# Small steps of a norm and of a softmax rewritten, and elementwise work moved from GpSimd to VectorE, in a two-layer encoder kernel

## The chip, the cores and the metric

The kernel runs on one core of one Trainium2 chip. A core has a matrix engine (TensorE, PE in the profile, with its weight loads shown as PEld), VectorE (DVE), ScalarE (ACT), GpSimd (POOL) and a queue that issues most DMAs (SyncE, SP). The engines share an on-chip memory, SBUF, of 128 partitions; PE writes its results to PSUM, eight banks that DVE and ACT can read and write. The metric is the device time of one execution in microseconds (us); lower is better.

## The reference

Two requests, a prompt of 512 tokens and a sample of 1024, go through two layers with the same weights. All numbers are float32.

```python
def trunk(x, p, ln1, w_in, sink, w_fmix, w_ao, w_fo, w_out, w_pe, ln_pg, w_pg, ln_f):
    h = x
    for i in range(DEPTH):                       # DEPTH = 2, D_MODEL = 1024
        z = rmsnorm(h, ln1[i]) @ w_in[i]         # 1024 -> 4352 columns
        q, k, v, ga, uf, gf, mga, mgf = jnp.split(z, SPLIT_IDX, axis=-1)
        ...                                      # partial rotary on q and k
        a = band_attention(q, k, v, sink[i]) * jax.nn.silu(ga)
        f = fourier_mix(uf, w_fmix[i]) * jax.nn.silu(gf)
        merged = jax.nn.sigmoid(mga) * (a @ w_ao[i]) + jax.nn.sigmoid(mgf) * (f @ w_fo[i])
        h = h + merged @ w_out[i]
        gate = jax.nn.sigmoid(rmsnorm(h, ln_pg[i]) @ w_pg[i])
        h = h + (p[i].astype(h.dtype) @ w_pe[i]) * gate
    return rmsnorm(h, ln_f)

# in band_attention, s holds one head's scores times 1/8, masked to |i-j| <= 128:
    m = jnp.maximum(jnp.max(s, axis=-1, keepdims=True), sk)
    e = jnp.exp(s - m)
    pr = e / (jnp.sum(e, axis=-1, keepdims=True) + jnp.exp(sk - m))
```

## The kernel before

The tokens lie in three chunks of 512: chunk 0 is the prompt, chunks 1 and 2, the pair, are the sample. Activations stand transposed, 128 channels by 512 tokens to a tile. Every product is made of three matmuls of rounded operands: each operand is split into a high part, a cast on ACT (`S.copy`, L86), and a low part, the difference (L87), on the engine that the caller names (`hi_lo`). Those two lines are most of what ACT, DVE and POOL do.

A layer runs these stages, one after the other on PE, with side work stepped in between by `run`:

- `project_prompt`: 34 weight tiles times chunk 0 (L98 to L100). `Weights` loads a tile two steps ahead and splits it one step ahead, in two halves, on the two engines in `engs`. In layer 0 these are POOL and DVE; the streams of all later stages name POOL twice. Beside it run the norm and the operands of the pair (`pair_made`), the prompt's attention and its Fourier mixing.
- `project_pair`: 17 pairs of weight tiles times both sample chunks by a scheme with seven products in place of eight (`Pair`, L231). For each pair four sums of weight blocks S1 to S4 are made (L208 to L215, on POOL) and seven blocks are split, their low parts by turns on POOL (four) and on DVE (three). Each product goes to one of three PSUM banks, which DVE and ACT empty (L238 to L260). The sample's attention runs beside it.
- `merge` for the prompt, then for the pair: the branches' projections with gates (L514 to L522, whose sum is on POOL), the output projection with the residual (L540) and the sum of squares for the next norm (L299, L300), and the gate with its embedding (L556 to L560). The sample's Fourier mixing runs beside the first of them.

`Norm` adds up squares tile by tile (L300, on POOL where the caller names no engine). `stats` has PE turn the sums to a 128x4 tile in a PSUM bank (L305) and finds 1/sqrt by an integer guess and three rounds of three small operations (L307 to L314), all in SBUF tiles. `scale` has PE spread the result over a bank (L320), and DVE copies it out (L322).

In `attention`, one unit is a block of 128 queries and one key-value head, with four query heads. For each head DVE adds the mask to the scores and takes the row maximum (L675), makes the bias of it, at most minus the sink (L678), and ACT takes the exponential with its row sum (L680). After four heads the sink's share is made and added (L683 to L685), the reciprocal taken (L686) and the rows scaled (L688).

What sets the order: the program is written as generators, and the framework's scheduler then orders each engine's instructions by times that it expects. Each engine runs its own list strictly in that order, so an instruction that waits holds up all behind it.

Of the kernel before, what the change touches and what calls it, by code (L numbers as in the profile page):

```python
# [10 lines left out]
F32 = mybir.dt.float32  # L11
# [7 lines left out]
P = 128  # L19
# [20 lines left out]
def trunk(ctx: ExitStack, tc: tile.TileContext, x, p, w_in, w_af, w_out, w_pe, w_pg, w_fm,  # L40
# [14 lines left out]
    def sbt(shape, dt, tag, bufs=None):  # L55
        return sb.tile(shape, dt, tag=tag, name=nm(tag), bufs=bufs or BUFS[tag])
# [27 lines left out]
    def hi_lo(hi, lo, src, lo_eng):  # L84

        S.copy(hi, src)  # L86
        lo_eng.tensor_tensor(lo, src, f(hi), op=ALU.subtract)  # L87
# [93 lines left out]
    class Pair:  # L181
# [19 lines left out]
        def prepare(self, n):  # L201

            for b in range(len(self.w), min(n + 1, 7 * (len(self.sources) // 2))):
                p, i = divmod(b, 7)
                a, name = self.a[p], self.ORDER[i]
                if name == "S2":
                    a["S1"], a["S2"] = sbt([P, 4, P], F32, "scr"), sbt([P, 4, P], F32, "scr")
                    G.tensor_tensor(a["S1"], a["A21"], a["A22"], op=ALU.add)  # L208
                    G.tensor_tensor(a["S2"], a["S1"], a["A11"], op=ALU.subtract)
                elif name == "S3":  # L210
                    a["S3"] = sbt([P, 4, P], F32, "scr")
                    G.tensor_tensor(a["S3"], a["A11"], a["A21"], op=ALU.subtract)
                elif name == "S4":
                    a["S4"] = a["S2"]
                    G.tensor_tensor(a["S4"], a["A12"], a["S2"], op=ALU.subtract)  # L215
                t = wt([P, 2, 4, P], F32R)
                hi_lo(t[:, 0], t[:, 1], a[name], V if i % 2 else G)
                self.w[b] = [(t[:, 0, k, :], t[:, 1, k, :]) for k in range(4)]

        def steps(self, p, x, finish, lead):  # L220
# [68 lines left out]
    class Norm:  # L289
        def __init__(self):  # L290
            self.acc = None

        def add(self, h, eng=G):
            if self.acc is None:
                self.acc = scr()
                S.activation(self.acc, h, AF.Square)
            else:
                sq = scr()
                S.activation(sq, h, AF.Square)  # L299
                eng.tensor_tensor(self.acc, self.acc, sq, op=ALU.add)  # L300

        def stats(self):
            st = pst("misc")
            for j in range(4):
                PE.matmul(st[:, j : j + 1], self.acc[:, j * P : (j + 1) * P], mean_sb, start=True, stop=True)  # L305
            v, r, z = (sbt([P, 4], F32, "tiny") for _ in range(3))
            V.tensor_scalar(v, st[:, 0:4], EPS, None, op0=ALU.add)  # L307

            V.tensor_scalar(r.bitcast(I32), v.bitcast(I32), 1, None, op0=ALU.arith_shift_right)
            V.tensor_scalar(r.bitcast(I32), r.bitcast(I32), -1.0, float(0x5F3759DF), op0=ALU.mult, op1=ALU.add)  # L310
            for _ in range(3):
                V.scalar_tensor_tensor(z, r, -0.5, r, op0=ALU.mult, op1=ALU.mult)
                V.tensor_tensor(z, z, v, op=ALU.mult)
                V.scalar_tensor_tensor(r, z, 1.5, r, op0=ALU.add, op1=ALU.mult)  # L314
            self.r = r

# [182 lines left out]
    def merge(l, chunks, parts, ws, bank, groups):  # L499
# [3 lines left out]
        for m in range(KD):  # L503
            w = ws.get()
            for c in chunks:
                ga, gf = scr(), scr()
                SY.dma_start(ga, GT[c][2 * m])
                SY.dma_start(gf, GT[c][2 * m + 1])
                ao, fo = bank(), bank()
                mm3(ao, w[:4], parts[c][:4])  # L510
                tick()
                yield
                mm3(fo, w[4:], parts[c][4:])
                V.scalar_tensor_tensor(ga, ga, 1.0, ao, op0=ALU.add, op1=ALU.mult)  # L514
                V.scalar_tensor_tensor(gf, gf, 1.0, fo, op0=ALU.add, op1=ALU.mult)
                if len(chunks) == 1:
                    G.tensor_tensor(gf, ga, gf, op=ALU.add)
                    outs[c].append(two(halves(gf, V)))
                else:
                    if m % 2 == 0:  # L520
                        merged[c].append(big([P, 2, T]))
                    G.tensor_tensor(merged[c][-1][:, m % 2, :], ga, gf, op=ALU.add)  # L522
                yield
        if len(chunks) > 1:
            for c in chunks:
# [106 lines left out]
    def attention(l, chunks, slim):  # L632
# [25 lines left out]
        def scores(u):  # L658
            c, b, kv = units[u]
            qb, k0, k1 = window(c, b)  # L660
            W = (k1 - k0) * P
            msk = mask_sb[:, (k0 - qb + 1) * P : (k1 - qb + 1) * P]
            q, kw = blocks[c, b][kv]["q"], blocks[c, b][kv]["kw"]
            mx, nmx, rs, es, rd = (sbt([P, 4], F32, "stat") for _ in range(5))
            probs = []
            for i in range(4):
                head = 4 * kv + i
                sc = pst("sc")
                for j in range(2):
                    PE.matmul(sc[:, :W], q[:, i, :], kw[:, j, :], start=j == 0, stop=j == 1)  # L670
# [4 lines left out]
                V.tensor_tensor_reduce(out=pr, in0=sc[:, :W], in1=msk, scale=1.0, scalar=-3.0e38,  # L675
                                       op0=ALU.add, op1=ALU.max, accum_out=mx[:, e])

                V.scalar_tensor_tensor(nmx[:, e], mx[:, e], -0.125, nsink_sb[:, l, head : head + 1],  # L678
                                       op0=ALU.mult, op1=ALU.min)
                S.activation(pr, pr, AF.Exp, bias=nmx[:, e], scale=0.125, accum_out=rs[:, e])  # L680
                if i % 2:
                    yield
            V.tensor_tensor(es, sink_sb[:, l, 4 * kv : 4 * kv + 4], nmx, op=ALU.add)  # L683
            S.activation(es, es, AF.Exp)
            V.tensor_tensor(rd, rs, es, op=ALU.add)  # L685
            V.reciprocal(rd, rd)  # L686
            for i, pr in enumerate(probs):
                S.activation(pr, pr, AF.Copy, scale=rd[:, i : i + 1])  # L688
            blocks[c, b][kv]["probs"] = probs

        def values(u):
# [53 lines left out]
    def fourier(l, s):  # L745
# [68 lines left out]
        for g in range(4):  # L814
# [61 lines left out]
            o = tile([P, n_tok])  # L876
            V.tensor_copy(o[:, 0:1], s1[:, 0:1])
            V.tensor_tensor(o[:, 1 : quart + 1], s1[:, 1:], t1, op=ALU.subtract)
            G.tensor_tensor(o[:, 3 * quart :], s1[:, quart:0:-1], t1[:, ::-1], op=ALU.add)
            V.tensor_tensor(o[:, quart + 1 : half], s2[:, quart - 1 : 0 : -1], t2[:, quart - 2 :: -1], op=ALU.add)  # L880
            V.tensor_copy(o[:, half : half + 1], s2[:, 0:1])
            G.tensor_tensor(o[:, half + 1 : 3 * quart], s2[:, 1:quart], t2[:, : quart - 1], op=ALU.subtract)
            yield
            for i, c in enumerate(chunks):
                gu = gus[i]
# [222 lines left out]
```

## Time and profile before

| what | value |
|---|---|
| time, median of 3 runs | 2336.91 us (2334.51 to 2337.52) |
| profiled execution | 2336.8 us, its span 2334.6 us |
| PE busy | 2211.7 us, 10176 matmuls |
| DVE, ACT, POOL busy | 1424.6, 1088.9, 1113.4 us |

The span runs from the first to the last instruction; about 2.2 us lie outside it. Matmuls overlap in the profile, so PE's busy time is the time in which at least one is under way, and its idle time is the rest of the span, 122.9 us. The row PEclk of the page tells which share of full speed the chip granted to PE's clock. A row of a timeline reads: start, time from the first start to the last end, engine, line, operation, written tile, read tiles, sizes, number of instructions, and in brackets the idle time before and what ended it.

### The profile page before, as it was taken

Reading aid. Unit: us, or ns where it says so; the run is one execution under the profiler, and the core shown is the slowest. Engines: PE = TensorE matmul, PEld = TensorE weight load, DVE = VectorE, ACT = ScalarE, POOL = GpSimd, SP = SyncE. Lnnn points to the kernel's source line nnn. Section 1 sums busy time; section 2 is a strip of 40 time slices with the busy share of each in tenths; the row PEclk is TensorE's granted clock in tenths of the full one; section 3 lists DMA queues with packets and bytes.
Section 4 is the critical chain, followed back from the end, with each engine's and each line's share of the span. In section 5 each row is a group of like instructions: output and inputs, shape, how many; then the busy total and the mean of one; then the engine's idle time right before and its main releaser. Section 6 shows DMA issues by size and latency. Waiting matters only on the chain. (4 is left out here: it accounts for less than half of the span.)

```text
span 2334.6 us, 30544 instructions
## 1 busy us (share of the span) xinstructions
PE 2211.7 (95%) x10176; PEld 1812.2 (78%) x10176; DVE 1424.6 (61%) x2563; ACT 1088.9 (47%) x2292; POOL 1113.4 (48%) x827
## 2 busy tenths in 40 slices
PE   8899999999998989999999999899999999999986
PEld 6677777888877877888887787788787788788875
DVE  5866645677566775252767653657766666744376
ACT  5467433466664444223424853336666544422331
POOL 1313446444446863344514355644444568554471
PEclk9899999999999999999999999999999999999998
DMA  7565435445437464731445554453444655553232
GB/s 280 187 198 177 164 119 178 147 140 165 131 130 269 153 237 163 249 117 47 140 166 185 153 177 168 149 171 125 148 154 132 218 198 186 198 194 117 87 113 95
DMA packets 240542, 380.73 MB, mean 163 GB/s; under 512 B 21121, under 2 KB 95489, under 8 KB 240385
## 3 DMA queue, kind: packets, MB, share of 16 engines
q1 hardware_dynamic: 233472, 366.19, 46.6%
q10 hardware_dynamic: 6912, 12.59, 1.5%
q8 instruction: 81, 1.33, 0.2%
q14 instruction: 77, 0.62, 0.1%
HBM read 270.17 MB, written 108.53 MB: 162 GB/s over the span
## 5 line engine op out<-in xcount | busy, mean ns | idle before, releaser
L87 POOL TENSOR_TENSOR act<-act,act 128x512 fp32r<-128x512 f32 x386 | 547.2, 1437 | 463.4 <-ACT act L86 403.8
L231 PE MATMUL mm<-act,act 128*128 128x512 f32 x2856 | 700.4, 395 | 27.6 <-DVE act L87 11.7
L231 PEld LDWEIGHTS mm<-act,act 128*128 128x128 f32 x2856 | 531.1, 189 | 147.2 <-ACT act L86 18.0
L98 PE MATMUL mm<-act,act 128*128 128x512 f32 x1408 | 563.1, 400 | 29.6 <-ACT act L86 28.5
L100 PE MATMUL mm<-act,act 128*128 128x512 f32 x1408 | 559.3, 399 | 13.2 <-POOL act L87 13.2
L99 PE MATMUL mm<-act,act 128*128 128x512 f32 x1408 | 557.8, 396 | 0.0
L86 ACT CAST act<-act 128x512 fp32r<-128x512 f32 x574 | 330.1, 619 | 223.0 <-DMA act<-in_w_af 53.2
L98 PEld LDWEIGHTS mm<-act,act 128*128 128x128 f32 x1408 | 269.8, 192 | 88.6 <-ACT act L86 35.0
L100 PEld LDWEIGHTS mm<-act,act 128*128 128x128 f32 x1408 | 269.3, 191 | 78.2 <-POOL act L87 23.4
L99 PEld LDWEIGHTS mm<-act,act 128*128 128x128 f32 x1408 | 269.7, 192 | 54.0
L87 DVE TENSOR_TENSOR act<-scr,act 128x512 fp32r<-128x512 f32 x188 | 180.7, 979 | 102.8 <-ACT act L86 101.6
L86 ACT CAST act<-scr 128x512 fp32r<-128x512 f32 (+1 forms) x260 | 152.6, 614 | 170.8 <-DVE scr L382 79.0
L87 POOL TENSOR_TENSOR act<-scr,act 128x512 fp32r<-128x512 f32 (+1 forms) x72 | 100.1, 1392 | 207.6 <-ACT act L86 141.1
L87 DVE TENSOR_TENSOR act<-act,act 128x512 fp32r<-128x512 f32 x188 | 172.2, 944 | 35.7 <-ACT act L86 34.7
L300 POOL TENSOR_TENSOR scr<-scr,scr 128x512 f32<-128x512 f32 x67 | 94.5, 1411 | 173.5 <-ACT scr L299 164.1
L299 ACT ACTIVATE scr<-act 128x512 f32<-128x512 f32 x105 | 65.3, 632 | 236.8 <-DVE act L540 148.1
L680 ACT ACTIVATE act<-act,stat 128x384 f32<-128x384 f32 (+1 forms) x192 | 111.0, 580 | 68.9 <-DVE stat L678 68.5
L87 DVE TENSOR_TENSOR act<-misc,act 128x512 fp32r<-128x512 f32 x132 | 88.5, 687 | 76.8 <-ACT act L86 76.3
L86 ACT CAST act<-misc 128x512 fp32r<-128x512 f32 x132 | 73.7, 586 | 96.1 <-PE misc L707 93.6
L675 DVE CUSTOM_DVE_ANT_0 act<-sc,mask_sb 128x384 f32<-128x384 f32 (+1 forms) x192 | 92.4, 508 | 41.8 <-PE sc L670 36.7
L100 PE MATMUL sc<-act,act 128*128 128x512 f32 (+1 forms) x292 | 111.8, 383 | 1.1 <-DVE act L87 1.1
L98 PE MATMUL sc<-act,act 128*128 128x512 f32 (+1 forms) x292 | 111.5, 383 | 0.0
(209 smaller groups left out, 3019.3 us busy)
## 6 DMA issues: line engine op xcount, KB each, us to landing
act<-in_w_in SPq DMA_DIRECT2D x136, 256.0 KB, 4.3
act<-in_w_in SPq DMA_DIRECT2D x68, 512.0 KB, 4.7
gt<-scr SPq DMA_DIRECT2D x96, 256.0 KB, 2.3
scr<-gt SPq DMA_DIRECT2D x96, 256.0 KB, 5.3
act<-in_w_pg SPq DMA_DIRECT2D x80, 256.0 KB, 3.7
act<-in_w_af SPq DMA_DIRECT2D x64, 256.0 KB, 4.8
act<-in_w_out SPq DMA_DIRECT2D x64, 256.0 KB, 4.9
pl<-scr ACTq DMA_DIRECT2D x48, 256.0 KB, 2.5
```

The costliest lines, as they stand in the source:

```text
L86: S.copy(hi, src)
L87: lo_eng.tensor_tensor(lo, src, f(hi), op=ALU.subtract)
L98: PE.matmul(out, wh, xh, start=i == 0, stop=False)
L99: PE.matmul(out, wh, xl, start=False, stop=False)
L100: PE.matmul(out, wl, xh, start=False, stop=i == n - 1)
L231: PE.matmul(bank, w, v, start=first and k == 0 and n == 0, stop=k == 3 and n == 2, skip_group_check=True)
L299: S.activation(sq, h, AF.Square)
L300: eng.tensor_tensor(self.acc, self.acc, sq, op=ALU.add)
L675: V.tensor_tensor_reduce(out=pr, in0=sc[:, :W], in1=msk, scale=1.0, scalar=-3.0e38, op0=ALU.add, op1=ALU.max, accum_out=mx[:, e])
L680: S.activation(pr, pr, AF.Exp, bias=nmx[:, e], scale=0.125, accum_out=rs[:, e])
```

## The change

The results are the same sums, computed in other places and in another form:

- `Norm.stats` keeps its intermediate values v, y and z in unused columns of the PSUM bank that holds the sums; only r stays in SBUF. Each round is v times r, then times -0.5 r, then plus 1.5 times r, so no step reads two SBUF tensors. There are still twelve steps.
- In attention the scores are scaled by -1/8 while the mask is added, and the minimum is taken over the row and minus the sink in the same instruction (the scalar of L675 is now a column of `nsink_sb`); its result is the bias. One more column with minus the sink is put behind each row (a copy on ACT for two heads), so the exponential's row sum contains the sink's share. L678, L683, L684 and L685 go.
- From POOL to DVE go: the sums S1 to S4 and the four low parts of each pair; the first halves' low parts of layer 0's first weights; the squares' sums where no engine is named; the sum in `merge`; two of the six assembled pieces in the Fourier mixing. POOL keeps the low parts of the later weight streams, and what else names it.

```diff
@@ class Pair, prepare
-                    G.tensor_tensor(a["S1"], a["A21"], a["A22"], op=ALU.add)
-                    G.tensor_tensor(a["S2"], a["S1"], a["A11"], op=ALU.subtract)
+                    V.tensor_tensor(a["S1"], a["A21"], a["A22"], op=ALU.add)
+                    V.tensor_tensor(a["S2"], a["S1"], a["A11"], op=ALU.subtract)
...
-                hi_lo(t[:, 0], t[:, 1], a[name], V if i % 2 else G)
+                hi_lo(t[:, 0], t[:, 1], a[name], V)
@@ class Norm
-        def add(self, h, eng=G):
+        def add(self, h, eng=V):
...
-            v, r, z = (sbt([P, 4], F32, "tiny") for _ in range(3))
+            v, y, z = (st[:, 4 * j : 4 * j + 4] for j in range(1, 4))
+            r = sbt([P, 4], F32, "tiny")
             V.tensor_scalar(v, st[:, 0:4], EPS, None, op0=ALU.add)
-            V.tensor_scalar(r.bitcast(I32), v.bitcast(I32), 1, None, op0=ALU.arith_shift_right)
-            V.tensor_scalar(r.bitcast(I32), r.bitcast(I32), -1.0, float(0x5F3759DF), op0=ALU.mult, op1=ALU.add)
+            V.tensor_scalar(y.bitcast(I32), v.bitcast(I32), 1, None, op0=ALU.arith_shift_right)
+            V.tensor_scalar(r.bitcast(I32), y.bitcast(I32), -1.0, float(0x5F3759DF), op0=ALU.mult, op1=ALU.add)
             for _ in range(3):
-                V.scalar_tensor_tensor(z, r, -0.5, r, op0=ALU.mult, op1=ALU.mult)
-                V.tensor_tensor(z, z, v, op=ALU.mult)
+                V.tensor_tensor(z, v, r, op=ALU.mult)
+                V.scalar_tensor_tensor(z, z, -0.5, r, op0=ALU.mult, op1=ALU.mult)
                 V.scalar_tensor_tensor(r, z, 1.5, r, op0=ALU.add, op1=ALU.mult)
@@ merge
-                    G.tensor_tensor(gf, ga, gf, op=ALU.add)
+                    V.tensor_tensor(gf, ga, gf, op=ALU.add)
...
-                    G.tensor_tensor(merged[c][-1][:, m % 2, :], ga, gf, op=ALU.add)
+                    V.tensor_tensor(merged[c][-1][:, m % 2, :], ga, gf, op=ALU.add)
@@ attention, scores
-                    t = big([P, 2, W])
+                    t = big([P, 2, W + 1])
+                    S.copy(t[:, :, W], nsink_sb[:, l, head : head + 2])
                 pr, e = t[:, i % 2, :], slice(i, i + 1)
-                V.tensor_tensor_reduce(out=pr, in0=sc[:, :W], in1=msk, scale=1.0, scalar=-3.0e38,
-                                       op0=ALU.add, op1=ALU.max, accum_out=mx[:, e])
-                V.scalar_tensor_tensor(nmx[:, e], mx[:, e], -0.125, nsink_sb[:, l, head : head + 1],
-                                       op0=ALU.mult, op1=ALU.min)
-                S.activation(pr, pr, AF.Exp, bias=nmx[:, e], scale=0.125, accum_out=rs[:, e])
+                V.tensor_tensor_reduce(out=pr[:, :W], in0=sc[:, :W], in1=msk, scale=-0.125,
+                                       scalar=nsink_sb[:, l, head : head + 1],
+                                       op0=ALU.add, op1=ALU.min, accum_out=nmx[:, e])
+                S.activation(pr, pr, AF.Exp, bias=nmx[:, e], scale=-1.0, accum_out=rs[:, e])
...
-            V.tensor_tensor(es, sink_sb[:, l, 4 * kv : 4 * kv + 4], nmx, op=ALU.add)
-            S.activation(es, es, AF.Exp)
-            V.tensor_tensor(rd, rs, es, op=ALU.add)
-            V.reciprocal(rd, rd)
+            V.reciprocal(rd, rs)
@@ fourier
-            G.tensor_tensor(o[:, 3 * quart :], s1[:, quart:0:-1], t1[:, ::-1], op=ALU.add)
+            V.tensor_tensor(o[:, 3 * quart :], s1[:, quart:0:-1], t1[:, ::-1], op=ALU.add)
...
-            G.tensor_tensor(o[:, half + 1 : 3 * quart], s2[:, 1:quart], t2[:, : quart - 1], op=ALU.subtract)
+            V.tensor_tensor(o[:, half + 1 : 3 * quart], s2[:, 1:quart], t2[:, : quart - 1], op=ALU.subtract)
@@ trunk
-    ws = Weights(w_ins(0), (G, V))
+    ws = Weights(w_ins(0), (V, V))
```

Three places show how the engines' lists stand. The first is DVE's list at the norm of chunk 1 in the last gate stage (the rows give line, operation, written tile, read tiles, size; `misc` is a PSUM bank, `tiny` an SBUF tile). Before:

```order
L307 TENSOR_SCALAR tiny_19950<-misc_19945 128x4
L309 TENSOR_SCALAR tiny_19951<-tiny_19950 128x4
L310 TENSOR_SCALAR tiny_19951<-tiny_19951 128x4
L312 SCALAR_TENSOR_TENSOR tiny_19952<-tiny_19951 128x4
L313 TENSOR_TENSOR tiny_19952<-tiny_19952,tiny_19950 128x4
L314 SCALAR_TENSOR_TENSOR tiny_19951<-tiny_19952,tiny_19951 128x4
```

In the changed kernel, at the same place:

```order
L309 TENSOR_SCALAR misc_19587<-misc_19587 128x4
L311 TENSOR_SCALAR misc_19587<-misc_19587 128x4
L312 TENSOR_SCALAR tiny_19592<-misc_19587 128x4
L314 TENSOR_TENSOR misc_19587<-misc_19587,tiny_19592 128x4
L315 SCALAR_TENSOR_TENSOR misc_19587<-misc_19587,tiny_19592 128x4
L316 SCALAR_TENSOR_TENSOR tiny_19592<-misc_19587,tiny_19592 128x4
```

The number of steps is the same, and each of them now has a PSUM tile among what it reads.

The second place is the start of layer 0's `project_pair`. DVE's list before, from the emptying of the second bank (L242) to the next one (L248):

```order
L242 TENSOR_TENSOR scr_3096<-mm_3057,scr_3079 128x512
L87 TENSOR_TENSOR act_3042<-act_610,act_3042 128x512
L87 TENSOR_TENSOR act_3045<-act_612,act_3045 128x512
L87 TENSOR_TENSOR act_3064<-scr_3062,act_3064 128x512
L87 TENSOR_TENSOR act_3103<-act_2905,act_3103 128x512
L248 TENSOR_TENSOR scr_3134<-mm_3057,scr_3079 128x512
```

The changed kernel's DVE list there:

```order
L242 TENSOR_TENSOR scr_3034<-mm_2995,scr_3017 128x512
L87 TENSOR_TENSOR act_2980<-act_608,act_2980 128x512
L87 TENSOR_TENSOR act_2983<-act_610,act_2983 128x512
L87 TENSOR_TENSOR act_2997<-scr_2920,act_2997 128x512
L87 TENSOR_TENSOR act_3002<-scr_3000,act_3002 128x512
L87 TENSOR_TENSOR act_3019<-act_2842,act_3019 128x512
L87 TENSOR_TENSOR act_3041<-act_2843,act_3041 128x512
L87 TENSOR_TENSOR act_3057<-scr_2921,act_3057 128x512
L87 TENSOR_TENSOR act_3074<-act_3037,act_3074 128x512
L248 TENSOR_TENSOR scr_3072<-mm_2995,scr_3017 128x512
```

Four low parts that POOL made (two of weight sums, two of weight blocks) have come into DVE's list between the two emptyings.

The third place is one unit of the prompt's attention in layer 0 on DVE, from its third head on (ISA is the masked maximum and the read of its result). Before:

```order
L675 ISA act_1170,stat_1133<-sc_1167,mask_sb 128x256
L675 ISA stat_1133 128x1
L675 ISA act_1170,stat_1133<-sc_1174,mask_sb 128x256
L675 ISA stat_1133 128x1
L87 TENSOR_TENSOR act_1157<-act_1076,act_1157 128x512
L678 SCALAR_TENSOR_TENSOR stat_1134<-stat_1133,nsink_sb 128x1 x2
L683 TENSOR_TENSOR stat_1136<-sink_sb,stat_1134 128x4
L685 TENSOR_TENSOR stat_1137<-stat_1135,stat_1136 128x4
```

In the changed kernel (its L680 is L675 before):

```order
L680 ISA act_1161,stat_1127<-sc_1158,mask_sb,nsink_sb 128x256
L680 ISA stat_1127 128x1
L680 ISA act_1161,stat_1127<-sc_1165,mask_sb,nsink_sb 128x256
L680 ISA stat_1127 128x1
L686 RECIPROCAL stat_1129<-stat_1128 128x4
```

The bias comes straight from the masked minimum, and the reciprocal follows with no step between.

More of the change, by code (lines that the diff above doesn't have):

```diff
@@ L207, in prepare @@
                     a["S1"], a["S2"] = sbt([P, 4, P], F32, "scr"), sbt([P, 4, P], F32, "scr")
-                    G.tensor_tensor(a["S1"], a["A21"], a["A22"], op=ALU.add)
-                    G.tensor_tensor(a["S2"], a["S1"], a["A11"], op=ALU.subtract)
+                    V.tensor_tensor(a["S1"], a["A21"], a["A22"], op=ALU.add)
+                    V.tensor_tensor(a["S2"], a["S1"], a["A11"], op=ALU.subtract)
                 elif name == "S3":
                     a["S3"] = sbt([P, 4, P], F32, "scr")
-                    G.tensor_tensor(a["S3"], a["A11"], a["A21"], op=ALU.subtract)
+                    V.tensor_tensor(a["S3"], a["A11"], a["A21"], op=ALU.subtract)
                 elif name == "S4":
                     a["S4"] = a["S2"]
-                    G.tensor_tensor(a["S4"], a["A12"], a["S2"], op=ALU.subtract)
+                    V.tensor_tensor(a["S4"], a["A12"], a["S2"], op=ALU.subtract)
                 t = wt([P, 2, 4, P], F32R)
-                hi_lo(t[:, 0], t[:, 1], a[name], V if i % 2 else G)
+                hi_lo(t[:, 0], t[:, 1], a[name], V)
                 self.w[b] = [(t[:, 0, k, :], t[:, 1, k, :]) for k in range(4)]
@@ L663, in scores @@
             q, kw = blocks[c, b][kv]["q"], blocks[c, b][kv]["kw"]
-            mx, nmx, rs, es, rd = (sbt([P, 4], F32, "stat") for _ in range(5))
+            nmx, rs, rd = (sbt([P, 4], F32, "stat") for _ in range(3))
             probs = []
@@ L671, in scores @@
                 if i % 2 == 0:
-                    t = big([P, 2, W])
+                    t = big([P, 2, W + 1])
+                    S.copy(t[:, :, W], nsink_sb[:, l, head : head + 2])
                 pr, e = t[:, i % 2, :], slice(i, i + 1)
                 probs.append(pr)
-                V.tensor_tensor_reduce(out=pr, in0=sc[:, :W], in1=msk, scale=1.0, scalar=-3.0e38,
-                                       op0=ALU.add, op1=ALU.max, accum_out=mx[:, e])
-                V.scalar_tensor_tensor(nmx[:, e], mx[:, e], -0.125, nsink_sb[:, l, head : head + 1],
-                                       op0=ALU.mult, op1=ALU.min)
-                S.activation(pr, pr, AF.Exp, bias=nmx[:, e], scale=0.125, accum_out=rs[:, e])
+                V.tensor_tensor_reduce(out=pr[:, :W], in0=sc[:, :W], in1=msk, scale=-0.125,
+                                       scalar=nsink_sb[:, l, head : head + 1],
+                                       op0=ALU.add, op1=ALU.min, accum_out=nmx[:, e])
+                S.activation(pr, pr, AF.Exp, bias=nmx[:, e], scale=-1.0, accum_out=rs[:, e])
                 if i % 2:
                     yield
-            V.tensor_tensor(es, sink_sb[:, l, 4 * kv : 4 * kv + 4], nmx, op=ALU.add)
-            S.activation(es, es, AF.Exp)
-            V.tensor_tensor(rd, rs, es, op=ALU.add)
-            V.reciprocal(rd, rd)
+            V.reciprocal(rd, rs)
             for i, pr in enumerate(probs):
-                S.activation(pr, pr, AF.Copy, scale=rd[:, i : i + 1])
+                S.activation(pr[:, :W], pr[:, :W], AF.Copy, scale=rd[:, i : i + 1])
             blocks[c, b][kv]["probs"] = probs
```

## The prediction

> **What bounds the kernel now.** I read the page's busy times first, then whom PE waited for, then groups of instructions by line, and last the timelines at PE's long waits.
>
> ```profile
> PE 2211.7 (95%) x10176; PEld 1812.2 (78%) x10176; DVE 1424.6 (61%) x2563; ACT 1088.9 (47%) x2292; POOL 1113.4 (48%) x827
> ```
>
> PE has work for 95% of the span, and the change adds and removes no matmul. So what it can win is PE's idle time, 2334.6 - 2211.7 = 122.9 us, and time in which matmuls run at a reduced clock. PE's waits (total, times, longest):
>
> ```profile
> PE mm L98 <- ACT act L86: 28.5, 12, 7.6
> PE mm L100 <- POOL act L87: 13.2, 21, 1.7
> PE misc L320 <- DVE tiny L314: 13.0, 4, 6.2
> PE mm L231 <- DVE act L87: 11.7, 8, 2.2
> PE misc L305 <- DVE scr L300: 10.4, 2, 7.2
> ...
> PE mm L231 <- POOL act L87: 3.7, 2, 1.9
> ...
> PE mm L231 <- DVE stat L685: 2.5, 2, 1.2
> ...
> PE sc L670 <- DVE stat L675: 1.9, 4, 0.9
> ...
> PE mm L231 <- DVE scr L260: 1.0, 2, 0.6
> ```
>
> About half of it ends with a DVE or POOL operation. The groups tell why those are late (after the bar: busy us, mean ns of one; then idle time):
>
> ```profile
> L87 POOL TENSOR_TENSOR act<-act,act 128x512 fp32r<-128x512 f32 x386 | 547.2, 1437 | 463.4 <-ACT act L86 403.8 <-DVE act L87 11.6 <-DMA act<-k 10.3
> ...
> L87 DVE TENSOR_TENSOR act<-scr,act 128x512 fp32r<-128x512 f32 x188 | 180.7, 979 | 102.8 <-ACT act L86 101.6
> L87 DVE TENSOR_TENSOR act<-act,act 128x512 fp32r<-128x512 f32 x188 | 172.2, 944 | 35.7 <-ACT act L86 34.7 <-DMA act<-in_w_in 0.3
> L300 POOL TENSOR_TENSOR scr<-scr,scr 128x512 f32<-128x512 f32 x67 | 94.5, 1411 | 173.5 <-ACT scr L299 164.1 <-DMA act<-in_w_pg 4.6 <-PE mm L100 2.8
> L87 DVE TENSOR_TENSOR act<-misc,act 128x512 fp32r<-128x512 f32 x132 | 88.5, 687 | 76.8 <-ACT act L86 76.3
> L678 DVE SCALAR_TENSOR_TENSOR stat<-stat,nsink_sb 128x1 f32<-128x1 f32 x192 | 82.5, 446 | 1.2
> ...
> L208 POOL TENSOR_TENSOR scr<-act 128x512 f32<-128x512 f32 x34 | 45.7, 1345 | 0.0
> ...
> L684 ACT ACTIVATE stat<-stat 128x4 f32<-128x4 f32 x48 | 9.5, 199 | 6.0 <-DVE stat L683 6.0
> ```
>
> The same subtraction takes DVE 687 ns where one input is in PSUM (`misc`), and 979 or 944 where both are in SBUF. These two SBUF groups alone lose 188 x (979 - 687) + 188 x (944 - 687) = 103 us. A step on one element a partition (L678) takes 446. The timeline of the last gate stage shows what such steps wait for:
>
> ```profile
> 2215.10 18.29 POOL L87 TENSOR_TENSOR act<-act,act 128x512 fp32r<-128x512 f32 x14
> ...
> 2217.49 0.16 DVE L307 TENSOR_SCALAR tiny<-misc 128x4 f32<-128x4 f32 x1
> 2217.69 0.88 DVE L309 TENSOR_SCALAR tiny<-tiny 128x4 int32<-128x4 int32 x1
> ...
> 2229.76 1.19 DVE L314 SCALAR_TENSOR_TENSOR tiny<-tiny,tiny 128x4 f32<-128x4 f32 x1
> ...
> 2231.09 1.09 PE L320 MATMUL misc<-ident_sb,tiny 128*128 128x128 f32 x4 [6.21 <-DVE tiny L314]
> ```
>
> POOL subtracts without a break, 18.29 / 14 = 1.3 us each, and the norm's SBUF steps take about that long each; only L307, which reads PSUM, takes 0.16. At the kernel's end POOL is idle, and the whole chain is short:
>
> ```profile
> 2320.42 0.16 DVE L307 TENSOR_SCALAR tiny<-misc 128x4 f32<-128x4 f32 x1 [2.02 <-PE misc L305]
> 2320.61 0.17 DVE L309 TENSOR_SCALAR tiny<-tiny 128x4 int32<-128x4 int32 x1
> ...
> 2322.59 0.16 DVE L314 SCALAR_TENSOR_TENSOR tiny<-tiny,tiny 128x4 f32<-128x4 f32 x1
> ...
> 2322.90 1.09 PE L320 MATMUL misc<-ident_sb,tiny 128*128 128x128 f32 x4 [2.52 <-DVE tiny L314]
> ```
>
> **The norm's steps in PSUM.** With an input in PSUM a step doesn't wait for POOL (L307, and L87 at 687), so the chain takes 2322.75 - 2320.42 = 2.3 us wherever it stands. No DVE step here writes PSUM; I bound it by L307's 0.16 below, since the shortest rows are all of that size, and by L678's 0.446 above, and take 0.16, the same kind of step. Twelve steps then take 2.3 to 5.4 us. Started at 2217.49 they end by 2222.9 even so; PE came to L320 at 2231.09 - 6.21 = 2224.88, so the wait of **6.2** goes whole. The other long one:
>
> ```profile
> 855.63 0.15 DVE L307 TENSOR_SCALAR tiny<-misc 128x4 f32<-128x4 f32 x1
> ...
> 864.63 1.11 PE L320 MATMUL misc<-ident_sb,tiny 128*128 128x128 f32 x4 [4.14 <-DVE tiny L314]
> ```
>
> With one 0.69 subtraction in between the chain ends at 858.6 (at 861.7 by the upper bound); PE came at 860.49, so **4.1** goes (2.9 by the bound). The 2.52 at the end stays, up to 3.1 more by the bound. Behind long waits PE runs slowly for a while (stretch, length, then busy us of PE, PEld, DVE, ACT, POOL with counts, granted clock, DMA share, GB/s):
>
> ```profile
> 2229.60:2236.30 6.70, 5.21 (x15) 4.29 (x16) 3.03 (x5) 1.15 (x2) 6.70 (x7) 0.50 0.33 114
> ...
> 717.50:720.70 3.20, 3.20 (x9) 2.52 (x8) 1.11 (x3) 0.00 (x0) 2.72 (x2) 0.50 1.02 410
> 864.30:867.50 3.20, 2.87 (x9) 2.49 (x10) 3.13 (x7) 0.00 (x0) 0.00 (x0) 0.50 0.21 63
> ```
>
> At a granted clock of 0.50 a matmul holds PE for twice its time: the kernel's mean is 2211.7 / 10176 = 0.22, so the 15 and 9 matmuls behind these two waits lose 24 x 0.2 = **4.8**, which goes with the waits.
>
> [...]
>
> **The pair's sums and splits.** Four sums (1345 ns, L208) and four low parts (1437) of each of 34 pairs leave POOL. On DVE I take 0.69 each, the 687 row, 5.5 us a pair; 0.98 is the upper bound. DVE in the two stretches of `project_pair` (columns as above):
>
> ```profile
> 316.00:716.00 400.00, 383.99 (x1783) 313.61 (x1782) 264.25 (x491) 222.33 (x479) 197.48 (x145) 1.00 0.46 152
> ...
> 1462.00:1852.00 390.00, 376.88 (x1752) 308.07 (x1753) 255.09 (x481) 215.79 (x467) 193.33 (x142) 1.00 0.45 146
> ```
>
> It is busy 264 of 400 us. It gains 17 x 5.5 = 94, loses its share of the 103 (400 / 2335, 18) and L678 for a third of the units (82.5 / 3 = 27): 313, 78%. So DVE doesn't become the bound, though more is queued ahead of each step. PE's waits there:
>
> ```profile
> 326.01 5.29 PE L231 MATMUL mm<-act,act 128*128 128x512 f32 x22 [1.94 <-DVE act L87]
> ...
> 710.57 3.47 PE L231 MATMUL mm<-act,act 128*128 128x512 f32 x14 [1.87 <-POOL act L87]
> ...
> 716.21 2.37 PE L231 MATMUL mm<-act,act 128*128 128x512 f32 x7 [2.17 <-DVE act L87]
> ```
>
> Layer 1 repeats them (totals 11.7 and 3.7 above). At 326 DVE's four subtractions stop colliding (up to 4 x 0.3 by the means, more in a full collision) and four more join: I take 1.5 of 1.94. At 710 1.44 becomes 0.69, and nothing else is ahead of it on POOL: 1.0 of 1.87. At 716 the next stage's weight splits, which stay on POOL, still collide: 0.5. Twice 3.0 is **6.0**; bounds 0 and 12.
>
> The stretch at 717.5 ran at 0.50 behind a wait of 2.17, so a shorter wait there may win 9 x 0.2 = 1.8, twice; I count nothing. [...]
>
> **Attention.** The shorter L231 waits on DVE (11.7 - 2 x (1.94 + 2.17) = 3.5), L685 (2.5) and L675 (1.9), 7.9 together, hang on its small steps. L678 and L685 go and the rest collides less; the masked minimum stays: **5.0**, bounds 0 and 7.9. The minimum's scalar is now a column: nothing, or at worst the 0.45 of the step that it replaces. ACT makes 96 copies and no longer 48 of L684, 0.2 us each, and may wait where DVE wrote the buffer first. In the prompt's attention that counts:
>
> ```profile
> 140.00:200.00 60.00, 57.09 (x291) 45.97 (x291) 39.33 (x126) 49.30 (x125) 11.29 (x9) 1.00 0.50 160
> ```
>
> ACT is busy 82% there; 16 units of 0.2 more make 0 to 3.2, and I take **-1.6**.
>
> **What else leaves POOL**: 42 squares, 48 merge sums, 34 first splits, 32 short pieces. POOL mostly waits for ACT's casts (403.8 of 463.4 idle), so only a low part that stood behind such an operation comes earlier: **3.0** of L100's 13.2, bounds 0 and 10. Against it stands the start:
>
> ```profile
> 68.53 1.76 DVE L87 TENSOR_TENSOR act<-scr,act 128x512 fp32r<-128x512 f32 x1
> ...
> 69.80 0.50 PE L100 MATMUL mm<-act,act 128*128 128x512 f32 x1 [0.91 <-POOL act L87]
> ```
>
> The awaited low part now follows DVE's at 68.53, which ends at 70.3: 70.3 + 0.69 = 71.0, **-1.2**.
>
> **The sum.** 6.2 + 4.1 + 4.8 + 6.0 + 5.0 + 3.0 = 29.1, less 1.6 and 1.2, and less 2 because DVE empties banks later (L260's 1.0, tripled for a queue twice as long): -24.3. From the profiled execution, 2336.8, that gives 2312.5, predicted **2312**; the median of the runs, 2336.91, is the same. The waits for ACT (28.5) and at the end (7.2) I leave: nothing that is moved stands in their way.
>
> **The rivals.**
> - *DVE takes POOL's place.* A bank is emptied in DVE's order, behind eight low parts where four stood, and a sum whose weights are late holds up all behind it. Two extra operations ahead of one emptying cost 1.4 us a pair, 34 x 1.4 = 47: 2312 + 47 = 2359, slower; it decides from 24 / 34 = 0.7 us a pair. For it: eight operations a pair join a strict queue. Against it: at 66% these emptyings cost PE 1.0 in all. Chance 0.09.
> - *Only the norm gains.* Other freed time ends in the next wait, mostly ACT's casts: 2336.8 - 15.1 + 4.8 = 2326, 0.16; with reordered lists eating that too, about 2336, 0.08.
> - *More goes.* The rest of the pair starts (6), attention (2.9), L100 (10.2), a third of ACT's 28.5 (9.5) and the 3.6 of clock: 2312 - 32 = 2280. Casts that stand behind a DVE step speak for it. Chance 0.13.
> - *The steps in PSUM are held up too*: 2312 + 15 = 2327. L307's 0.16 in a run of 1.2 speaks against it. Chance 0.02.
>
> **How the numbers follow.** The forecast, 2300 to 2322, has 0.52. The range 2288 to 2336 takes in *only the norm*, the bounds at the end (3.1) and on ACT, and the nearer part of *more goes*; 0.2 are left out. A measurement of this kernel can tell about 0.2%, 4.7 us, from no change: faster by more 0.52 + 0.16 + 0.13 + 0.02 = 0.83, within it 0.08, slower 0.09.
>
> **What would show it.** Right: L322 (L320 before) waits some 3 us in all, the half-speed stretches behind it are gone, DVE's L87 from two SBUF inputs falls to 700 to 850 ns, POOL to some 530 us busy, and L231's waits for DVE are under 8 together. Wrong: PE waits for L242 to L260 by tens of us, or its waits for ACT grow by what the others lose.

## The result, and the profile after

| | before | after |
|---|---|---|
| time, median | 2336.12 us (4 runs, 2334.51 to 2337.52) | 2284.26 us (4 runs, 2281.18 to 2286.77) |
| span of the profiled execution | 2334.6 us | 2284.5 us |
| PE idle in it | 122.9 us | 87.8 us |
| mean granted clock | 0.980 | 0.978 |

The ratio is 0.9778, with a 95% interval of 0.9761 to 0.9795: faster by 52 us, more than twice the forecast's 24 and 4 us beyond the low end of its range. The busy times of the changed kernel, from its page:

```profile
PE 2196.7 (96%) x10176; PEld 1816.5 (80%) x10176; DVE 1457.6 (64%) x2703; ACT 1089.9 (48%) x2340; POOL 556.0 (24%) x399
```

POOL lost half of its busy time and DVE gained only 33 us. PE's busy time fell by 15.0 us too, with the same matmuls at no better clock. Its waits (total, times, longest):

```profile
PE mm L98 <- ACT act L86: 30.7, 9, 7.4
PE misc L305 <- DVE scr L300: 8.8, 3, 7.4
PE mm L100 <- POOL act L87: 5.5, 5, 2.5
...
PE mm L231 <- ACT act L86: 5.0, 6, 1.7
PE mm L100 <- DVE act L87: 3.2, 3, 2.1
PE misc L707 <- ACT act L688: 2.9, 2, 1.5
PE misc L322 <- DVE tiny L316: 2.6, 1, 2.6
...
PE mm L231 <- DVE scr L248: 1.8, 2, 0.9
PE mm L231 <- DVE act L87: 1.4, 2, 0.7
```

L322 stands where L320 had 13.0, and L231's waits for DVE's low parts fell from 11.7 to 1.4, those for POOL's from 3.7 to none; the waits for ACT's casts at L98 stayed. DVE's groups after (busy us, mean ns), and the masked minimum:

```profile
L87 DVE TENSOR_TENSOR act<-act,act 128x512 fp32r<-128x512 f32 x290 | 207.9, 747 | 50.5 <-ACT act L86 50.0
L87 DVE TENSOR_TENSOR act<-scr,act 128x512 fp32r<-128x512 f32 x256 | 192.1, 771 | 63.4 <-ACT act L86 62.1
L680 DVE CUSTOM_DVE_ANT_0 act<-sc,mask_sb,nsink_sb 128x384 f32<-128x384 f32 (+1 forms) x192 | 103.9, 569 | 51.7 <-PE sc L672 38.8
```

The same subtraction fell from 979 (from `scr`) and 944 ns to 771 and 747, towards the 687 that it takes with one input in PSUM. The norm at the last gate stage, in the changed kernel's timeline:

```profile
2173.61 0.17 DVE L309 TENSOR_SCALAR misc<-misc 128x4 f32<-128x4 f32 x1 [0.90 <-PE misc L305]
2173.82 0.17 DVE L311 TENSOR_SCALAR misc<-misc 128x4 int32<-128x4 int32 x1
...
2175.83 0.16 DVE L316 SCALAR_TENSOR_TENSOR tiny<-misc,tiny 128x4 f32<-128x4 f32 x1
```

The chain takes 2175.99 - 2173.61 = 2.4 us there, where it had kept PE waiting until 2231 before.

Why PE's busy time can fall: two matmuls in a row of the same timeline.

```profile
2184.02 0.39 PE L98 MATMUL sc<-act,act 128*128 128x512 f32 x1
2184.25 0.39 PE L99 MATMUL sc<-act,act 128*128 128x512 f32 x1
```

A matmul is shown for 0.39 us and the next starts after 0.23. So the first 0.16 us of each wait lies under the matmul ahead of it and counts as busy, and a wait shorter than that isn't listed at all. Measured from start to start over all 10176 matmuls, the delays of 60 ns and more beyond the closest spacing, without stretches at half clock, fell by some 50 us, which is the whole gain. (By one choice of the closest spacing they went from 168 to 117; other choices move both numbers and give falls of 45 to 55.) The loss at half clock did not fall (24.9 and 27.0 by the same choice).

### The profile page after: what moved, and what is told of

Same layout as the page of the kernel before. It is cut to its first block, busy times and chain, and to the rows that moved or that the text cites. A ratio compares the mean times of both kernels' runs of the same rounds, so it can differ in the third digit from the quotient of the medians.

```text
span 2284.5 us, 30071 instructions
## 1 busy us (share of the span) xinstructions
PE 2196.7 (96%) x10176; PEld 1816.5 (80%) x10176; DVE 1457.6 (64%) x2703; ACT 1089.9 (48%) x2340; POOL 556.0 (24%) x399
## 4 chain that ended last, share of the span: by engine, by line
PE 82%; DVE 8%; ACT 3%; DMA 3%; issue 3%; POOL 1%; SPq 1%; DVEq 0%; ACTq 0%; POOLq 0%
PE mm L231 26%; PE mm L100 12%; PE mm L98 12%; PE mm L99 11%; PE o L712 3%; PE sc L100 3%; PE sc L98 3%; PE sc L99 3%; PE sc L672 2%; PE misc L707 2%; ACT act L86 1%; DVE act L329 1%; DVE act L87 1%; PE o L99 1%; PE o L100 1%
## 5 line engine op out<-in xcount | busy, mean ns | idle before, releaser
L231 PE MATMUL mm<-act,act 128*128 128x512 f32 x2856 | 698.6, 395 | 8.3 <-ACT act L86 5.0
L231 PEld LDWEIGHTS mm<-act,act 128*128 128x128 f32 x2856 | 534.2, 189 | 122.2 <-ACT act L86 10.7
L98 PE MATMUL mm<-act,act 128*128 128x512 f32 x1408 | 563.1, 400 | 32.6 <-ACT act L86 30.7
L100 PE MATMUL mm<-act,act 128*128 128x512 f32 x1408 | 559.4, 399 | 8.9 <-POOL act L87 5.5
L87 POOL TENSOR_TENSOR act<-act,act 128x512 fp32r<-128x512 f32 x284 | 403.3, 1447 | 548.6 <-ACT act L86 452.5
L98 PEld LDWEIGHTS mm<-act,act 128*128 128x128 f32 x1408 | 269.8, 192 | 88.1 <-ACT act L86 34.0
L100 PEld LDWEIGHTS mm<-act,act 128*128 128x128 f32 x1408 | 269.2, 191 | 70.4 <-POOL act L87 8.8
L87 DVE TENSOR_TENSOR act<-act,act 128x512 fp32r<-128x512 f32 x290 | 207.9, 747 | 50.5 <-ACT act L86 50.0
L87 DVE TENSOR_TENSOR act<-scr,act 128x512 fp32r<-128x512 f32 x256 | 192.1, 771 | 63.4 <-ACT act L86 62.1
L721 POOL TENSOR_TENSOR scr<-scr,scr 128x512 f32<-128x512 f32 x24 | 34.6, 1440 | 769.4 <-DVE scr L718 769.4
L87 DVE TENSOR_TENSOR act<-misc,act 128x512 fp32r<-128x512 f32 x132 | 88.2, 687 | 77.2 <-ACT act L86 76.8
L680 DVE CUSTOM_DVE_ANT_0 act<-sc,mask_sb,nsink_sb 128x384 f32<-128x384 f32 (+1 forms) x192 | 103.9, 569 | 51.7 <-PE sc L672 38.8
L683 ACT ACTIVATE act<-act,stat 128x385 f32<-128x385 f32 (+1 forms) x192 | 110.8, 580 | 48.1 <-DVE stat L680 47.5
L100 PE MATMUL sc<-act,act 128*128 128x512 f32 (+1 forms) x292 | 111.2, 381 | 0.9 <-DVE act L87 0.9
L98 PE MATMUL sc<-act,act 128*128 128x512 f32 (+1 forms) x292 | 111.0, 381 | 0.0
L99 PE MATMUL sc<-act,act 128*128 128x512 f32 (+1 forms) x292 | 110.7, 380 | 0.0
```

The costliest lines, as they stand in the source:

```text
L98: PE.matmul(out, wh, xh, start=i == 0, stop=False)
L99: PE.matmul(out, wh, xl, start=False, stop=False)
L100: PE.matmul(out, wl, xh, start=False, stop=i == n - 1)
L231: PE.matmul(bank, w, v, start=first and k == 0 and n == 0, stop=k == 3 and n == 2, skip_group_check=True)
L680: V.tensor_tensor_reduce(out=pr[:, :W], in0=sc[:, :W], in1=msk, scale=-0.125, scalar=nsink_sb[:, l, head : head + 1], op0=ALU.add, op1=ALU ...
L683: S.activation(pr, pr, AF.Exp, bias=nmx[:, e], scale=-1.0, accum_out=rs[:, e])
```

## The experiments

Four parts of the change were first made alone. The question was then whether what they give comes from DVE's steps no longer being held up (**theories A and M**: each wait goes by itself), only when the last of several causes goes (**B**), from the order in which the scheduler puts the lists of a kernel with other instructions (**C**), from the mere length of the chain from scores to exponential (**D**), from the sink's detour over ACT (**E**), or from POOL's late results alone (**P**). Each time stands beside the kernel before on the same chip; an interval of a ratio is about 0.0013 to each side, 3 us.

### One part at a time

Each kernel is the one before with one group of the diff's lines.

`e_norm`, `Norm.stats` alone:

> The kernel before with one part of the change: the norm's steps in PSUM. Theory A (DVE's steps from two SBUF tensors are held up by POOL, each part of the change frees its own waits, only the forecast's sizes were off): -10 to -15 us (forecast 15.1). In the trace of the whole change the step at the last gate stage moved by 8.9 and no clock gain was left over, so nearer -10. Theory B (a wait with several causes goes only when the last cause is gone, so the parts pay only together): -4 to -8. Theory C (the win comes from the new order of the engines' lists, not from the collision): any value, the four parts not adding up.

Measured 2327.6 (before 2336.1): -8.5. The profiled execution is the fastest of six that lie between 2323.5 and 2332.5. In its trace the step at the last gate stage is gone, but PE's waits for the squares (L305) are three instead of two, and it loses 3.4 us again between the 9900th matmul and the last.

`e_pair`, `Pair.prepare` alone:

> The kernel before with one part: the pairs' weight sums and four of seven low parts on DVE. Theory A: -18 to -26, since the two pair stages of the whole change gained 22 us, three times the forecast's 6, nearly all in the last third of each stage. Theory B: under 10, the rest of those 22 us needing the softmax and the squares as well. Theory C: no telling.

Measured 2321.0: -15.1, nearer to A than to B, against the forecast's 6.

`e_soft`, `scores` alone:

> The kernel before with one part: the softmax's bias by one row minimum and the sink as a column. Theory A: -3 to -6 (forecast 5.0 less 1.6 for the copies on ACT), in the prompt's attention and in the first two thirds of the pair stages. Theory B: within 2 us of before. Theory C: no telling.

Measured 2308.1: -28.0, far beyond the numbers of A and B; the forecast's 3.4 is an eighth of it.

`e_rest`, the remaining lines:

> The kernel before with one part: squares' sums, the sum in merge, the first weights' low parts and two Fourier pieces on DVE. Theory A: -8 to -12, by what is left of the 52 us when the other parts have theirs (forecast 3.0 less 1.2). Theory B: within 3 us of before. Theory C: no telling. The sum of the four parts: A 45 to 60, B under 35.

Measured 2322.5: -13.7. The sum of the four is 65, more than the whole's 52: the parts overlap, so B is out.

### Inside the softmax part

`s_bias` takes the bias from the minimum and keeps the sink's steps (the diffs of this part are against `e_soft`, and cut):

```diff
-                    t = big([P, 2, W + 1])
-                    S.copy(t[:, :, W], nsink_sb[:, l, head : head + 2])
+                    t = big([P, 2, W])
...
+            V.tensor_tensor(es, sink_sb[:, l, 4 * kv : 4 * kv + 4], nmx, op=ALU.add)
+            S.activation(es, es, AF.Exp)
+            V.tensor_tensor(rd, rs, es, op=ALU.add)
-            V.reciprocal(rd, rs)
+            V.reciprocal(rd, rd)
```

> The kernel before with half of the softmax part, which alone gave -28.0 us: the bias comes from the row minimum (192 steps of 128x1 go), while the sink keeps its own three steps per unit. Theory A (each such step is held up while POOL runs, and ACT's exponential waits for it): -12 to -20. Theory E (the sink's detour from DVE to ACT and back to DVE ahead of the reciprocal is what cost): under -8.

Measured 2319.4: -16.1 without the steps of 128x1, so the sink's detour has at most the other 12, each in its own lists. E is out as the main cause.

`s_two` puts such a step back behind the minimum:

```diff
+                V.scalar_tensor_tensor(bias[:, e], nmx[:, e], 1.0, nsink_sb[:, l, head : head + 1],
+                                       op0=ALU.mult, op1=ALU.min)
-                S.activation(pr, pr, AF.Exp, bias=nmx[:, e], scale=-1.0, accum_out=rs[:, e])
+                S.activation(pr, pr, AF.Exp, bias=bias[:, e], scale=-1.0, accum_out=rs[:, e])
```

> The kernel with the softmax part alone (2308.1 us), and again a step of 128x1 on two SBUF tensors between the row minimum and the exponential, which changes no value (192 in all). Theory A: it is held up as the old step was, mean some 450 ns, and gives back 12 to 20 of the 28 us. Theory D (the mere length of the chain counts, whatever the step reads): gives back the same as the step on PSUM. Theory E: gives back under 8.

`s_psum` has the same step with one input in PSUM:

```diff
+                V.scalar_tensor_tensor(bias[:, e], sc[:, 0:1], 0.0, nmx[:, e], op0=ALU.mult, op1=ALU.add)
```

> The same added step, but one of its two inputs is a column of the scores' PSUM bank (times 0). Theory A: some 160 ns each, not held up, gives back 0 to 6 us. Theory D: gives back as much as the step on two SBUF tensors, within 3 us.

Measured 2333.1 and 2334.9: each gives back 25 to 27 of the 28 us. Yet the steps themselves are as A says, by DVE's groups of `s_two`:

```profile
L681 DVE SCALAR_TENSOR_TENSOR stat<-stat,nsink_sb 128x1 f32<-128x1 f32 x192 | 82.5, 446 | 1.6
```

and of `s_psum`:

```profile
L681 DVE SCALAR_TENSOR_TENSOR stat<-sc,stat 128x1 f32<-128x1 f32 x192 | 25.6, 151 | 0.6
```

A step of 151 ns that is never held up cost as much as one of 446. So A alone fell. D was left, and C: with the added step, PE's list differs from `e_soft`'s, by tile names and sizes alone, in 461 (`s_two`) and 1023 (`s_psum`) of its 10176 places.

### The order held

To tell C from D, a kernel can be given the lists that the scheduler made for another one: after all instructions are written, each is tied behind the one that is to stand ahead of it on its engine. Such a tie, of the class `NoSync`, is there for the order alone.

```python
for k, d in enumerate(moved):
    i = own[k + d]
    e = str(i.engine)
    if e in ahead:
        tc.add_manual_dep(i, ahead[e].name, info, reason="order")
    ahead[e] = i
```

`moved` holds the places of the other kernel's plan; instructions that it doesn't have stand next to the one that they belong to. `h_psum` and `h_two` are `s_psum` and `s_two` in `e_soft`'s order, `h_rev` is `e_soft` in `s_two`'s (the code shown is that of the later `h_` kernels). In the traces, PE's matmuls then stand in the same order, by tile names and sizes, as in the kernel that the lists came from.

> The step on PSUM added to the softmax part cost 26.8 us (2308.1 to 2334.9), though it takes 151 ns and is never held up; so theory A is out for it. Here is the same kernel, with every engine's list held in the order of the kernel without the step (which stands behind its row minimum). Theory C (the scheduler plans another order when the step is there, and the order is what costs): 2308 to 2314. Theory D (the length of the chain from scores to exponential costs): 2328 to 2336.

> The same for the step on two SBUF tensors (2333.1 us in the scheduler's own order; mean 446 ns), in the order of the kernel without the step. Theory C: 2308 to 2316. Theory A with C: as much above the step on PSUM in the same order as 192 steps of 0.3 us more can cost, 3 to 15 us. Theory D: 2328 to 2336.

> The reverse: the softmax part without any added step (2308.1 us in its own order), with every engine's list held in the order that the scheduler made for the kernel with the step on two SBUF tensors. Theory C: 2326 to 2335. Theory D or A: 2306 to 2312.

| softmax part | `e_soft`'s lists | `s_two`'s lists | its own lists |
|---|---|---|---|
| no added step | 2308.1 | 2321.7 | 2308.1 |
| step on two SBUF tensors | 2320.9 | 2333.1 | 2333.1 |
| step on PSUM | 2312.2 | not run | 2334.9 |

The table adds up: the step on SBUF costs 12.8 or 11.4 us in the two lists, the lists cost 13.6 or 12.2 with either work, and the step that isn't held up costs 4.1, of the size of the interval. In `e_soft`'s lists the held-up step takes 380 ns on average and the other 158, so what is due to its being held up is the difference, 8.7 us. So D is out as the main cause, A is right for 9 to 13 us, and C for 12 to 14. The scheduler's own list is not the best for its work: `s_psum` runs 22.7 us faster in a list that was planned for another kernel.

### The whole change and its parts in the old lists

`h_after` is the whole change in the lists of before (PE's list is that of before to the instruction), `h_pair`, `h_rest` and `h_soft` the parts in the same lists, `h_back` the softmax part in the lists of the changed kernel.

> All parts of the change, with every engine's list held in the order of the kernel before (what goes from POOL to DVE stands in DVE's list at the place that it had in the joint plan; PE's list is that of before to the instruction). Theory M (the waits that go by themselves make most of the 52 us): 2284 to 2296. Theory C (the new lists make about half, as they did for the softmax part, 13.6 of 28): 2302 to 2314. By the forecast's own terms, which assume the old lists: 2312.

> The pair part alone (2321.0 us in its own lists) held in the lists of the kernel before. Theory M: 2319 to 2323, 15 us of gain stay. Theory C: the gain falls to the forecast's term of 6, 2328 to 2331.

> The rest part alone (squares, sum in merge, first weights, Fourier pieces; 2322.5 us in its own lists) held in the lists of the kernel before. Theory M: 2320 to 2325, 13 us of gain stay. Theory C: the gain falls to the forecast's 1.8 or at most 5, 2330 to 2335.

> The softmax part alone (2308.1 us in its own lists) held in the lists of the kernel before. From the step held up 192 times, which gave 11 to 13 us in either list: 2321 to 2325. If the sum of the parts in the old lists is to make the whole's 39: norm some 8, pair 17.3, rest 7.6, so 6 to 12 for the softmax, 2324 to 2330.

> The softmax part alone (2308.1 us in its own lists), held in the lists of the whole change: the norm on two SBUF tensors and POOL's work are as before. Theory M: near its own 2308, or later, 2305 to 2325. Theory C: the lists bring their share without the other parts, 2285 to 2300.

| gain in us | forecast | own lists | lists of before |
|---|---|---|---|
| norm | 15.1 | 8.5 | not run (its list differs in 55 places or more) |
| pair | 6.0 | 15.1 | 17.3 |
| softmax | 3.4 | 28.0 | 19.9 |
| rest | 1.8 | 13.7 | 7.6 |
| whole | 24.3 (2 taken off for later emptying) | 51.9 | 39.0 |

In the old lists the whole gives 39.0 us (2296.7, nearer to M than to C); the new lists bring the other 12.9. For the softmax part they are no gain by themselves: `h_back` (2319.4) is 11 us slower than the same work in its own lists, as M had it. `h_pair` (2318.4) is M's too, `h_rest` (2328.1) lies between the two, and `h_soft` (2315.9) gains more than I expected of it. With the norm's 8.5 the parts' sum in the old lists is 53, so 14 us are counted twice there. The reverse, the kernel before in the new lists, was not run.

Where the pair part's gain lies can be read wait by wait, since PE's list is the same. PE's waits in the last third of layer 0's `project_pair`, before:

```profile
PE mm L231 <- DVE act L87: 2.2, 1, 2.2
PE mm L231 <- POOL act L87: 1.9, 1, 1.9
PE mm L231 <- DVE stat L685: 1.2, 1, 1.2
PE o L712 <- ACT act L86: 1.1, 2, 0.6
PE mm L231 <- ACT act L86: 0.6, 1, 0.6
```

and the same matmuls in `h_pair`:

```profile
PE o L712 <- ACT act L86: 1.1, 2, 0.6
PE mm L231 <- DVE stat L685: 0.3, 1, 0.3
```

PE passes this third in 8.0 us less, in each layer. In layer 0 it loses 2.4 of them again right behind the stage, in a stretch of 6.8 us at half clock from 736.9 that the kernel before doesn't have there. At the stage's start in `h_pair`:

```profile
PE mm L231 <- DVE scr L252: 1.3, 1, 1.3
...
PE mm L231 <- DVE act L87: 0.4, 1, 0.4
```

The wait of 1.94 became 0.4, and a bank is emptied 1.3 later. For the softmax part, the stretch of the prompt's attention and Fourier mixing in layer 0, before (span, then busy us of PE, PEld, DVE, ACT, POOL with counts, granted clock, DMA share, GB/s):

```profile
140.00:316.00 176.00, 166.23 (x789) 135.90 (x789) 102.70 (x262) 100.67 (x254) 58.67 (x50) 0.95 0.49 162
```

and in `h_soft`:

```profile
140.00:310.00 170.00, 161.54 (x790) 132.62 (x789) 97.00 (x222) 98.99 (x255) 56.60 (x50) 0.98 0.51 167
```

About the same matmuls take 6 us less, and 4.7 of it is PE's busy time; its idle time went only from 9.8 to 8.5. The granted clock rose from 0.95 to 0.98, by which 0.05 x 176 = 8.8 us of lost clock became 0.02 x 170 = 3.4. Not all of the 6 us is clock: 3.2 come on the matmuls that ran from 140 to 200 before, at full clock in both kernels, and 2.8 on those from 222 to 240, where the half-speed stretch went.

`a_nosoft` is the whole change without its softmax part:

> The changed kernel (2284.3 us) with the softmax as before. The three other parts alone gave -8.5, -15.1 and -13.7. Theory A: with POOL relieved of half its work the old steps are held up less often (mean 200 to 300 ns instead of 446), so the softmax is worth 10 to 18 us here, 2294 to 2302. Theory D: its 28 us stay, 2312.

Measured 2297.9: as the last part to come, the softmax is worth 13.7 us, about half of its 28.0 alone. The old bias step (L678 before) takes 186 ns on average there, less than I expected and near the 150 of one that isn't held up, so little of these 13.7 can be its hold-up; what shares the sink's steps and the new lists have in them was not separated.

### POOL's load put back, and taken away

`h_twice` is the changed kernel, in its own lists, with the pairs' low parts made a second time on POOL:

```diff
                 hi_lo(t[:, 0], t[:, 1], a[name], V)
+                G.tensor_tensor(spare, a[name], f(t[:, 0]), op=ALU.subtract)
```

> The changed kernel (2284.3 us) in its own lists, with each of the pairs' 238 low parts made a second time on POOL into a tile that nobody reads; it leaves nothing out. Theory A (the collision costs): DVE's subtractions on two SBUF tensors in the pair stages rise from some 700 towards 1000 ns, and 8 to 17 us come back, 2292 to 2301. Theory P (only POOL's late results cost): within 3 us, 2281 to 2287.

Measured 2351.4: 67 us slower than the change, and slower than before (ratio 1.0072, 1.0059 to 1.0084). DVE's groups in it:

```profile
L87 DVE TENSOR_TENSOR act<-act,act 128x512 fp32r<-128x512 f32 x290 | 285.9, 1016 | 45.7 <-ACT act L86 43.8
L87 DVE TENSOR_TENSOR act<-scr,act 128x512 fp32r<-128x512 f32 x256 | 274.4, 1092 | 61.8 <-ACT act L86 60.3
```

and who PE waits for:

```profile
PE mm L234 <- DVE act L87: 18.1, 14, 2.8
PE mm L234 <- DVE scr L251: 11.0, 8, 2.5
...
PE mm L234 <- DVE stat L689: 6.3, 4, 1.7
```

The same work on DVE takes 1016 and 1092 ns instead of 747 and 771, and PE waits for DVE by tens of us. Layer 0's pair stage in the changed kernel (columns as above):

```profile
308.00:708.00 400.00, 393.44 (x1827) 324.68 (x1827) 282.67 (x530) 224.25 (x499) 25.03 (x17) 0.99 0.48 159
```

and in `h_twice`:

```profile
307.10:742.20 435.10, 405.45 (x1827) 325.02 (x1826) 368.35 (x532) 224.48 (x499) 211.49 (x134) 0.98 0.44 148
```

With POOL busy for 211 us, about what it had there before the change (202), DVE is busy for 368 us instead of 283 and the same matmuls take 35 us longer. In layer 1 it is 435 us instead of 402, so the two stages make up the whole loss. A is shown, several times larger than I expected, and P is out. A small part is not the collision: DVE waits 4.1 us and ACT 3.1 for tiles that POOL still reads, and PE's waits at L100 for POOL's low parts rise from 5.5 to 7.9. The rival *DVE takes POOL's place* looks like this: it happens when DVE has the work and POOL still collides with it.

`a_vv` has the later streams' low parts on DVE as well:

```diff
-        ws = Weights(streams(l) + ([] if last else w_ins(l + 1)), (G, G))
+        ws = Weights(streams(l) + ([] if last else w_ins(l + 1)), (V, V))
```

> The changed kernel (2284.3 us) with the low parts of all later weight streams on DVE as well, so that POOL keeps hardly anything. If freeing POOL is what gains: 2265 to 2280. If DVE's queue has become the bound or the order decides: 2284 to 2300.

Measured 2278.1, ratio to before 0.9757 (0.9744 to 0.9771): the best median of all, faster than before beyond doubt. Against the change (0.9761 to 0.9795) the intervals overlap slightly, so the 6 us are likely, not certain; and its lists are new too. At the same granted clock the runs of the two kernels lie 0 to 3 us apart (2283.3 and 2286.1 at 0.980, 2282.3 and 2282.4 at 0.982); the fastest of `a_vv`, 2277.1, had 0.986.

## Why the prediction was off

The direction and the mechanism were right: DVE's steps on SBUF tensors stood behind POOL's. The sum was less than half of what came. The step that failed most is the bound on what DVE's small steps in attention cost PE: it was taken from PE's listed waits, 7.9 us, and 5.0 of it was forecast where 19.9 came in the lists of before. The pair's 6.0 and the rest's 3.0 were mis-sized too, and the new lists stood in the sum at nothing, and in one rival as a loss, where they gave 12.9. By the prediction's own steps:

- **"What it can win is PE's idle time" and clock.** This bound hid half of the softmax's gain: in `e_soft` idle time fell by 13.3 us and busy time by 15.9. Short waits lie under the matmul ahead (the 0.16 us of the rows at 2184); some 5 of the 15.9 are clock (a mean granted clock of 0.980 before, of 0.982 in `e_soft`).
- **The norm's steps in PSUM.** Chain 2.3 us: 2.4 came. The 6.2 and 4.1 went whole, the 2.52 at the end stayed at 2.6. The clock term of 4.8 did not come as a gain: the half-speed stretch behind 2229 went, others appeared, and the total loss at half clock rose by 2. With the new wait for the squares the part alone gave 8.5, not 15.1.
- **The pair's sums and splits: 6.0, mis-sized; 17.3 in the lists of before.** The start at 326 gave 1.5 as forecast, and the later emptying took 1.3 of it. At 710 and 716, where I took 1.0 of 1.87 and 0.5 of 2.17, both waits went whole; with them went the clock behind 717, for which I counted nothing (in layer 0 a stretch at half clock came later instead), and part of the attention's waits. That is 8.0 a layer. The reason given for the 0.5, that the next stage's splits on POOL still collide, did not hold: in `h_pair` POOL starts them at 709.22, and DVE's last three subtractions, 0.6 to 0.7 us each, are over by 710.66.
- **Attention: 5.0 with bounds 0 and 7.9 less 1.6, the term that failed most.** 19.9 in the lists of before, 13.7 as the last part of the whole. The bound was the sum of PE's listed waits for DVE's small steps. It left out the clock in the prompt's attention, which rose from 0.95 to 0.98, and it left out L678, which ends no listed wait of PE's and yet was worth 11 to 13 us, 9 of them by its being held up (the table of `h_two` and `h_rev`). That it reaches PE by way of ACT's exponentials and transposes (L707, L712) fits, but no run isolates it.
- **What else leaves POOL: 3.0 less 1.2, mis-sized; 7.6 in the lists of before.** The loss at the start came as worked out: the wait at 69.80 went from 0.91 to 2.06. In the whole, L100's waits for POOL fell by 7.7 (3.2 for DVE came, the one at the start among them), and L305's first wait fell from 3.2 to 0.8, which I had left out.
- **DVE does not become the bound.** Right, and by more than I said: 71% of the pair stages, not 78%. L678, L683 and L685 took 51 us in the first of them and not the 27 that I credited for L678.
- **New lists.** I priced them nowhere in the sum, only as a reason for "about 2336". They brought 12.9 us of the 52. Which moves in them do it was not found out. The 2 that I took off for banks emptied later was mis-sized: PE's waits for them went from 1.0 (L260) to 1.8 (L248).
- **The rivals.** *More goes* (2280) was nearest in time, with wrong terms: ACT's 28.5 stayed (30.7), and L100 gave 7.7 of the 10.2. *The steps in PSUM are held up too* is out: L314 to L316 take 152 to 171 ns all 45 times.
- **What would show it.** L322 at 2.6, DVE's L87 at 747 and 771, POOL at 556, L231's waits for DVE at 3.2: all as forecast, while the time was off by 28 us. They showed the mechanism and said nothing on its size.

## What to carry to other kernels

Where an engine's small steps are held up, don't bound the gain by the listed waits of the engine that ends late (7.9 us of them here, and 19.9 gained): a wait is counted only beyond the overlap (0.16 us here), the granted clock can change too (from 0.95 to 0.98 in the prompt's attention), and freed steps shorten a whole chain (the norm's at the last gate stage from 13.5 us, 2217.49 to 2230.95, to 2.4). Price a change of a scheduled kernel with an uncertainty for the lists, here 2 to 23 us either way, and hold the lists to tell work from order. Part gains measured alone overlap (65 for 52), so the worth of a part is what it brings as the last one.

## What the runs showed of the hardware

DVE's small steps were held up until an instruction of POOL's ended: in the kernel before, each of the 138 that took more than 0.3 us (of L309 to L314, L678, L683 and L685) ends 10 to 26 ns after the end of one of POOL's. Steps on one SBUF tensor and an immediate were held up like those on two; before, L309 and L313 (fastest, median and slowest ns):

```profile
L309 DVE TENSOR_SCALAR tiny<-tiny x15: 170/171/1074, 29.0 to 2320.6; 128x4 int32<-128x4 int32 x15
...
L313 DVE TENSOR_TENSOR tiny<-tiny,tiny x45: 152/161/1224, 29.6 to 2322.4; 128x4 f32<-128x4 f32 x45
```

After, in PSUM:

```profile
L314 DVE TENSOR_TENSOR misc<-misc,tiny x45: 157/170/171, 29.2 to 2272.1; 128x4 f32<-128x4 f32 x45
```

The reciprocal of one SBUF tensor was not held up (161 to 180 ns in all 48 before, with POOL busy 48% of the time). What in the chip holds the steps up was not shown. The masked minimum with a column as its scalar takes 569 ns on average (L680 after), where it took 508 with a number (L675 before).
